# The hi part of each weight block from a rounding DMA in place of a ScalarE copy

## The chip, the cores and the metric

One Trainium2 chip, one of its cores. The metric is the device time of one execution in microseconds (us), as the median of several runs.

## The reference, cut to what matters

Two transformer-like blocks over 1024 tokens of width 1024, in float32. The first puts 16 meta tokens ahead, projects them all, runs three sequence mixers (HGRN2, Mamba2, S5), projects back, and ends in an MLP with a squared ReLU; the second has a gated delta rule, a spatial gating branch and a gated, convolved feed-forward. Around each stand layer norms. The dense products are what fills the time:

```python
proj = h @ w_in[l]                                        # 1040 x 1024 by 1024 x 3078
h = layer_norm(ALPHA * h + mixed @ w_out[l], ...)         # by 1024 x 1024
ff = jnp.square(jax.nn.relu(h @ w_mlp_in[l])) @ w_mlp_out[l]     # by 1024 x 4096 x 1024
proj = x @ w_in_2[l]                                      # by 1024 x 5128
h = gate_a * (o_a @ w_branch_a[l]) + gate_b * (o_b @ w_branch_b[l])
up = causal_depthwise_conv_2(x @ w_up[l], conv_ffn[l])    # by 1024 x 5632
x = ... (jax.nn.silu(a_ff) * b_ff) @ w_down[l]            # by 2816 x 1024
```

(The matrix sizes behind the comment signs are added here; in the kernel the tokens are taken in two halves.)

## The kernel before, in words

**Split operands.** A dense product in float32 is made of three products in float32r, the rounded form that TensorE takes in one pass: each operand is split into a hi part (the rounded value) and a lo part (what the rounding left), and `mm3` adds hi by hi, hi by lo and lo by hi in PSUM. Weights come from DRAM in blocks of 128 partitions by 1024 columns (512 KB; some are 780, 688 or 1032 columns wide). `weights` (line 223 on) does for each block: a DMA on SP's queue into a raw tile `wr` (2 buffers), a ScalarE copy into the float32r tile `wh` (3 buffers), and a VectorE subtraction raw - hi into `wl` (3 buffers):

```python
self.nc.sync.dma_start(raw[:, :w], src)
...
self.act(hi[:, :w], raw[:, :w])
self.tt(lo[:, :w], raw[:, :w], hi[:, :w].bitcast(F32), ALU.subtract)
```

There are 431 such blocks. A block feeds 24 products of 512 columns on TensorE, or about as much work; in the first projection, where some serve both halves, up to 72 shorter ones.

**How blocks are used.** In `fm` (first and second projection, the MLP's and feed-forward's up products, `merge`) a block is one unit: all its products, then the next block. In `down` (the MLP's and the feed-forward's products back to 1024 columns) blocks come in twos: for a group of four hidden tiles and each half `ch` of the output, two blocks A and B (then C and D) are both read in each of the four token tiles t = 0 to 3. With three buffers, C takes a buffer that was free before, while D takes A's, which is not read for the last time before the fourth token tile. There are 26 groups with four hidden tiles: 16 in the two halves of the MLP (`in_wmo`) and 10 in the feed-forward (`in_wdn`); two more have two.

**Stages.** `run` (line 1474 on) interleaves a dense part with the mixers' steps of another half by hand-written rates (`steps`). Roughly: up to 490 us the first projection, the mixers of the first half, its out-projection and the norm; from there to 2800 us the dense parts follow each other, with mixers beside them.

**Queues.** A scheduler orders the instructions of each engine by its own model of times; an engine then runs its list in order, and an instruction that waits holds up all behind it. In the kernel before, loads go on SP's queue, most stores of intermediates to DRAM (`S1`, `vdt`, `Y1`, `Y2`, `gt`, `qkv`, `sg` and the like) on GpSimd's (POOL), where there are also fills and the small power operation of the norms (line 1151). A few small loads are on ScalarE's queue.

Of the kernel before, what the change touches and what calls it, by code (L numbers as in the profile page):

```python
# [17 lines left out]
DRAM = bass.MemoryType.DRAM  # L18
# [6 lines left out]
ALPHA = 2.0 ** 0.25  # L25
# [4 lines left out]
# columns of the constant array  # L30
C_ID = 0
C_I10 = 128                   # 1024 times the identity
C_SGN = C_I10 + 128
C_TRI = C_SGN + 1
C_BLK = C_TRI + 128           # ones in the two diagonal 64-blocks
C_BAND = C_BLK + 128          # 64 zeros, 128 ones, 64 zeros
C_N = C_BAND + 256

# columns of the array of byte masks: the levels (only the columns in the second halves of their blocks),
# the same transposed (only the first halves), the diagonal, what is below it  # L40
# [6 lines left out]
# columns of the per-feature parameter array  # L47
P_HNW = 0
P_LB = 1
P_CW1 = P_LB + 3              # 7 x 4  # L50
# [4 lines left out]
P_CWQ = P_GB + 2              # 12 x 4  # L55
P_DNW = P_CWQ + 48
P_CWF = P_DNW + 1             # 44 x 3
# [4 lines left out]
# columns of the row array (the same on all partitions)  # L62
# [7 lines left out]
# order of the feature-major tiles of the first projection  # L70
U1 = dict(u=0, f=2, q=5, g=8, xbc=11, z=18)
NU1 = 21
# ... and of the second
# [4 lines left out]
class Op:  # L78
    """The hi and lo parts of an operand."""
# [8 lines left out]
class Kb:  # L88
# [54 lines left out]
    def mask(self, o, b=None):  # L143
        """A byte mask for four blocks of 128 columns, or for the halves of a level's blocks in them."""
        n = 128
        if b is not None:
            o += 64 * LEVELS.index(b)
            n = 64
        m = self.bm[:, o:o + n].rearrange("p (o t) -> p o t", o=1).to_broadcast([128, 4, n])
        return m if b is None else m.rearrange("p c (n b) -> p c n b", b=b)  # L150

    def halves(self, x, i, b):
        """The first or second halves of the blocks of 2 b columns."""
# [11 lines left out]
    def t(self, w, dt=F32):  # L165
        """A working tile of the mixers."""
        return self.mx.tile([128, 528], dt, tag="f", bufs=self.NF, name=self.nm("f"))[:, :w]

    def ta(self):
        """Two working tiles of 528 columns, out of the accumulators' tiles."""  # L170
# [16 lines left out]
    # ---------------------------------------------------------------- operands  # L187
# [18 lines left out]
    def xt(self, f=False):  # L206
        """A tile for the hi and lo parts of an operand; f: out of the mixers' tiles."""
# [8 lines left out]
    def split(self, src, w, f=False):  # L216
        """hi and lo parts of src [128, w]."""
# [5 lines left out]
    def weights(self, src, w):  # L223
        """hi and lo parts of a block of weights [128, w] in DRAM."""
# [4 lines left out]
        self.act(hi[:, :w], raw[:, :w])  # L229
# [3 lines left out]
    def mm3(self, out, a, b, start, stop):  # L233
        """out += a^T b with hi and lo parts."""
# [4 lines left out]
    def fm(self, out, w, xs, o, n, k0=0):  # L239
        """out [128 features, n tokens] from a unit of weights and the tiles xs."""  # L240
# [5 lines left out]
    # ---------------------------------------------------------------- first projection  # L246
    def p1(self):
# [21 lines left out]
        def unit(i, hs):  # L269
# [4 lines left out]
            for h in hs:  # L274
                if nme != "u":
                    self.S1[nme, j, h] = self.dram([128, HW[h] + 3], f"s{nme}{j}{h}")
                for o, n in pieces[h] if nme in ("u", "f", "xbc") or h == 1 else ((16, 512),):
# [3 lines left out]
                    if nme == "u":  # L281
# [3 lines left out]
                        nc.gpsimd.dma_start(self.uT[j][:, :, j0:j0 + n // 8],  # L285
# [3 lines left out]
                    nc.gpsimd.dma_start(self.S1[nme, j, h][:, 3 + o:3 + o + n], st[:, :n])  # L289
                    if nme == "xbc" and h == 0:  # L290
                        if o == 0:
                            nc.gpsimd.dma_start(self.S1[nme, j, 0][:, 0:3], self.zeros[:, 0:3])
                        else:
                            self.hx[j] = self.dram([128, 3], f"hx{j}")
                            nc.gpsimd.dma_start(self.hx[j], st[:, n - 3:n])
                    if nme == "xbc" and h == 1:
                        nc.gpsimd.dma_start(self.S1[nme, j, 1][:, 0:3], self.hx[j])
# [3 lines left out]
        def vd(h):  # L301
            tt = [(128 * c + T0[h], 128) for c in range(4)]
            for g in ([(0, 16)] + tt[:2], tt[2:]) if h == 0 else (tt,):
# [9 lines left out]
                for b, (o, n) in zip(bs, g):  # L313
                    st = self.ev()
                    self.act(st[:n, :390], b[:n, :390])
                    nc.gpsimd.dma_start(self.vdt[h][o:o + n, :], st[:n, :390])
# [21 lines left out]
    # ---------------------------------------------------------------- HGRN2  # L338
    def hgrn_pre(self):
        """ln(1 - lb) and lb, a column for each pair of heads."""  # L340
# [13 lines left out]
    def hgrn(self, p, h):  # L354
# [13 lines left out]
        # log f and k  # L368
# [19 lines left out]
        # scores  # L388
# [17 lines left out]
        # the queries of a level for both heads at once, each among zeros for the other's features  # L406
# [40 lines left out]
        # decays  # L447
# [12 lines left out]
        # kd with tokens on the partitions, and what each chunk adds to the state  # L460
# [16 lines left out]
        # the states before the chunks, both heads' on the diagonal  # L477
# [20 lines left out]
        # norm and gate  # L498
# [10 lines left out]
        nc.gpsimd.dma_start(self.Y1[h][p], r)  # L509

    # ---------------------------------------------------------------- Mamba2
    def softplus(self, x, tag, w):
        """max(x, 0) + ln(1 + exp(-|x|)) in place; x is narrow."""
# [6 lines left out]
    def rows(self, x, n):  # L520
        """The sums over tokens up to each, a row in DRAM for each of the n columns of x."""
# [15 lines left out]
    def square(self, x):  # L537
        """The hi and lo parts of the square of x [128, 512]."""
# [7 lines left out]
    def sums(self, out, parts):  # L546
        """The sum of the products of ones (lhsT) and operands (p: their partitions)."""
# [4 lines left out]
    def conv4(self, src, NT, cw, cb, out):  # L552
        """Causal convolution of four taps, then silu."""
# [10 lines left out]
    def mamba(self, h):  # L564
# [8 lines left out]
        # dt and dA, with tokens on the partitions; the first six columns are the short chunk  # L573
# [19 lines left out]
        for c in range(c0, 5):  # L593
            L = 16 if c == 0 else 128
            t0 = 0 if c == 0 else R0 + 128 * (c - 1)
            # acum_t and exp(acum_t) on all partitions
# [24 lines left out]
            # x dt and B with tokens on the partitions  # L621
# [39 lines left out]
        # gate, norm  # L661
# [9 lines left out]
        for j in range(3):  # L671
# [11 lines left out]
            nc.gpsimd.dma_start(self.Y1[h][3 + j], Y[j])  # L683
            yield

    # ---------------------------------------------------------------- S5
    def cmul(self, o, a, b, t):
        """o = a b for pairs (re, im) of access patterns; t: two temporaries of the shape."""
# [7 lines left out]
    def exp(self, out, x, w):  # L696
        """exp(x) to the last bits, for small tiles (w: four times the width of x)."""
# [1016 lines left out]
```

## Time and profile before

| | |
|---|---|
| median of 3 runs | 2840.28 us |
| lowest, highest | 2838.09, 2843.76 us |
| span of the profiled execution | 2831.3 us |
| median less that span | 9.0 us |
| PE (TensorE matmul) busy | 2768.6 us, 98% |
| DVE (VectorE) busy | 1793.7 us, 63% |
| ACT (ScalarE) busy | 1163.4 us, 41% |
| POOL (GpSimd) busy | 220.4 us, 8% |
| the 16 DMA engines, mean | 124 GB/s |

The profiled execution's own device time is not recorded apart from the three runs; its span, from the first to the last instruction, is what the rows below are read from, and 9.0 us is taken as what lies around it. A matmul's duration in a row is from its start to its modelled end, and matmuls overlap: what one costs in a full stretch is the stretch divided by their number.

### The profile page before, as it was taken

The page shows a single profiled execution, that of the slowest core. Times are in us where ns is not written, and L with a number is a line of the kernel's source. Part 1 is how long each engine was busy: PE and PEld are TensorE (multiplying, and loading weights), DVE is VectorE, ACT ScalarE, POOL GpSimd, SP SyncE. Part 2 cuts the span into 40 slices and gives each one's busy share as a digit, 9 for nine tenths or more (in the row PEclk, how much of TensorE's full clock was granted, in tenths as well). Part 3 has the DMA queues.
Part 4 walks back from the last instruction along what each step waited for, and adds up shares of the span by engine and source line. Part 5 has one row for each costly group of instructions (what it writes and reads, how often), then busy time and mean ns, then how long its engine had stood idle before and what let it go on. Part 6 is the DMA issues. An engine that isn't in the chain of part 4 may idle for free.

```text
span 2831.3 us, 37337 instructions
## 1 busy us (share of the span) xinstructions
PE 2768.6 (98%) x14176; PEld 2262.4 (80%) x14176; DVE 1793.7 (63%) x3321; ACT 1163.4 (41%) x1810; POOL 220.4 (8%) x365
## 2 busy tenths in 40 slices
PE   8999999999999999999999999999999999999997
PEld 7788777777878878877788888888788888888886
DVE  7678768777756554386545675535867557675556
ACT  4334344444442353364323334435545334344432
POOL 3121000000001121010000001110100000000000
PEclk9999999999999999999999999999999999999999
DMA  7333462323344444333333455433244433342232
GB/s 220 122 94 93 139 202 81 113 89 113 106 147 149 157 144 133 123 101 123 105 104 119 142 184 166 126 126 130 79 136 140 149 104 101 107 139 92 97 96 75
DMA packets 138036, 351.55 MB, mean 124 GB/s; under 512 B 26779, under 2 KB 40641, under 8 KB 137857
## 3 DMA queue, kind: packets, MB, share of 16 engines
q1 hardware_dynamic: 113712, 295.34, 32.9%
q0 software_dynamic: 16672, 48.50, 5.0%
q10 hardware_dynamic: 7473, 5.34, 0.7%
q8 instruction: 111, 1.82, 0.3%
q14 instruction: 68, 0.56, 0.1%
HBM read 296.84 MB, written 51.69 MB: 123 GB/s over the span
## 4 chain that ended last, share of the span: by engine, by line
PE 81%; issue 7%; DVE 6%; DMA 2%; ACT 2%; POOL 1%; SPq 0%; DVEq 0%; POOLq 0%; ACTq 0%
PE ps L204 73%; PE px L204 7%; DVE f L192 2%; ACT f L189 1%; DVE wl L192 1%; PE px L1265 1%; DVE f L195 1%; DMA hx<-ev 1%; DMA wr<-in_w 0%; DVE acc L195 0%; DMA f<-rows 0%; DVE f L433 0%; ACT wh L189 0%; DVE ta L192 0%; ACT ev L189 0%
## 5 line engine op out<-in xcount | busy, mean ns | idle before, releaser
L204 PE MATMUL ps<-xt,wh 128*128 128x512 f32 (+1 forms) x3616 | 1117.0, 388 | 8.7 <-ACT wh L189 8.5
L192 DVE TENSOR_TENSOR wl<-wr,wh 128x1024 fp32r<-128x1024 f32 (+3 forms) x431 | 521.5, 1210 | 606.7 <-ACT wh L189 590.2
L189 ACT ACTIVATE wh<-wr 128x1024 fp32r<-128x1024 f32 (+3 forms) x431 | 452.3, 1050 | 898.4 <-PE ps L204 826.1
L204 PE MATMUL ps<-wh,xt 128*128 128x512 f32 (+3 forms) x2624 | 813.1, 384 | 4.7 <-ACT xt L189 4.4
L204 PEld LDWEIGHTS ps<-xt,wh 128*128 128x128 f32 x3616 | 665.9, 189 | 141.7 <-ACT wh L189 8.5
L204 PE MATMUL ps<-xt,wl 128*128 128x512 f32 (+1 forms) x1808 | 698.6, 387 | 3.9 <-DVE wl L192 3.9
L204 PEld LDWEIGHTS ps<-wh,xt 128*128 128x128 f32 (+1 forms) x2624 | 485.8, 188 | 99.9 <-ACT xt L189 6.9
L204 PE MATMUL ps<-wl,xt 128*128 128x512 f32 (+3 forms) x1312 | 502.2, 383 | 0.8 <-DVE wl L192 0.7
L204 PEld LDWEIGHTS ps<-xt,wl 128*128 128x128 f32 x1808 | 341.5, 189 | 72.8 <-DVE wl L192 5.5
L204 PE MATMUL ps<-f,wh 128*128 128x512 f32 x960 | 300.5, 394 | 0.0
L204 PEld LDWEIGHTS ps<-wl,xt 128*128 128x128 f32 (+1 forms) x1312 | 246.7, 188 | 46.5 <-DVE wl L192 2.0
L189 ACT ACTIVATE f<-f 128x512 f32<-128x512 f32 (+6 forms) x300 | 178.5, 613 | 200.6 <-DVE f L192 62.3
L204 PE MATMUL px<-f,f 128*128 128x128 f32 (+8 forms) x1832 | 201.4, 258 | 16.8 <-DVE f L192 10.2
L204 PEld LDWEIGHTS ps<-f,wh 128*128 128x128 f32 x960 | 180.3, 188 | 42.3
L189 ACT ACTIVATE ev<-ps 128x512 f32<-128x512 f32 (+4 forms) x303 | 169.6, 561 | 72.9 <-PE ps L204 67.1
L192 DVE TENSOR_TENSOR acc<-acc,ps 128x512 f32<-128x512 f32 x192 | 130.8, 683 | 95.8 <-PE ps L204 93.9
L204 PE MATMUL ps<-f,wl 128*128 128x512 f32 x480 | 189.4, 394 | 0.0
L204 PEld LDWEIGHTS px<-f,f 128*128 128x128 f32 (+2 forms) x1192 | 133.3, 180 | 52.9 <-issue 22.8
L192 DVE TENSOR_TENSOR f<-f,f 128x256 f32<-128x256 f32 (+5 forms) x244 | 128.6, 547 | 39.0 <-ACT f L189 37.0
L189 ACT ACTIVATE xt<-ev 128x512 fp32r<-128x512 f32 x131 | 82.3, 629 | 149.2 <-DVE ev L192 145.9
L195 DVE SCALAR_TENSOR_TENSOR ev<-ev,p,ev 128x512 f32<-128x512 f32 x176 | 132.2, 751 | 2.7 <-ACT ev L189 0.6
L192 DVE TENSOR_TENSOR xt<-ev,xt 128x512 fp32r<-128x512 f32 x124 | 85.9, 696 | 49.6 <-ACT xt L189 49.1
(223 smaller groups left out, 2046.9 us busy)
## 6 DMA issues: line engine op xcount, KB each, us to landing
wr<-in_w SPq DMA_DIRECT2D x93, 512.0 KB, 3.8
wr<-in_wup SPq DMA_DIRECT2D x88, 512.0 KB, 3.5
wr<-in_wmi SPq DMA_DIRECT2D x64, 512.0 KB, 3.6
wr<-in_wmo SPq DMA_DIRECT2D x64, 512.0 KB, 3.6
wr<-in_wdn SPq DMA_DIRECT2D x44, 512.0 KB, 3.5
wr<-in_wo SPq DMA_DIRECT2D x32, 512.0 KB, 3.7
Y<-f POOLq DMA_DIRECT2D x32, 256.0 KB, 2.6
ev<-Y SPq DMA_DIRECT2D x32, 256.0 KB, 3.6
```

Source lines behind the costliest of these rows:

```text
L189: self.nc.scalar.activation(out=out, in_=in_, func=func, **kw)
L192: self.nc.vector.tensor_tensor(out=out, in0=a, in1=b, op=op)
L195: self.nc.vector.scalar_tensor_tensor(out=out, in0=a, scalar=s, in1=b, op0=op0, op1=op1)
L204: self.nc.tensor.matmul(out, lhsT, rhs, start=start, stop=stop)
L1265: nc.tensor.transpose(b[:, 128 * t:128 * t + 128], acc[t][:, 128 * k:128 * k + 128], self.ident)
```

## The change

`weights` fetches the block twice. The raw copy still comes on SP's queue. The hi part is no longer made by ScalarE: a second DMA, on POOL's queue, reads the same block from DRAM and writes it as float32r into `wh`, so that the transfer rounds. VectorE still subtracts. All stores that were on POOL's queue go to SP's. Buffers, loops and rates are as they were; comments and docstrings are taken out.

```diff
         raw = self.wp.tile([128, 1032], F32, tag="wr", bufs=2, name=self.nm("wr"))
         self.nc.sync.dma_start(raw[:, :w], src)
         hi = self.wp.tile([128, 1032], F32R, tag="wh", bufs=3, name=self.nm("wh"))
         lo = self.wp.tile([128, 1032], F32R, tag="wl", bufs=3, name=self.nm("wl"))
-        self.act(hi[:, :w], raw[:, :w])
+        self.nc.gpsimd.dma_start(hi[:, :w], src)
         self.tt(lo[:, :w], raw[:, :w], hi[:, :w].bitcast(F32), ALU.subtract)
...
-                    nc.gpsimd.dma_start(self.S1[nme, j, h][:, 3 + o:3 + o + n], st[:, :n])
+                    nc.sync.dma_start(self.S1[nme, j, h][:, 3 + o:3 + o + n], st[:, :n])
...
-            nc.gpsimd.dma_start(dst[:, o:o + 512], st[:, :512])
+            nc.sync.dma_start(dst[:, o:o + 512], st[:, :512])
```

The other stores (`uT`, `hx`, `vdt`, `Y1`, `Y2`, `X2`, `out`, `sg`, `qkv`) change in the same way.

The scheduler then places things anew. Three places:

**TensorE, `down` of a feed-forward group late in the program.** In the names, `wh_22358`/`wl_22359` are block A, `wh_22426` is C, and `wh_22432`/`wl_22433` are D, which takes A's buffer; `ps_22436`, `ps_22450` and `ps_22464` are the first three token tiles of the second half. In both kernels the last read of A stands 6 products ahead of the first read of C (six reads of B lie between). Before, D's first read follows after six products of C:

```order
L204 MATMUL ps_22436<-wh_22426,xt_21893 128x512
L204 MATMUL ps_22436<-wl_22427,xt_21893 128x512
L204 MATMUL ps_22436<-wh_22426,xt_21893 128x512
L204 MATMUL ps_22436<-wh_22426,xt_22110 128x512
L204 MATMUL ps_22436<-wl_22427,xt_22110 128x512
L204 MATMUL ps_22436<-wh_22426,xt_22110 128x512
L204 MATMUL ps_22436<-wh_22432,xt_22191 128x512
L204 MATMUL ps_22436<-wl_22433,xt_22191 128x512
```

Now there are ten of C ahead of it (the first six are the same as before, and the rows begin with the last of these):

```order
L204 MATMUL ps_22436<-wh_22426,xt_22110 128x512
L204 MATMUL ps_22450<-wh_22426,xt_21893 128x512
L204 MATMUL ps_22450<-wl_22427,xt_21893 128x512
L204 MATMUL ps_22450<-wh_22426,xt_21893 128x512
L204 MATMUL ps_22450<-wh_22426,xt_22110 128x512
L204 MATMUL ps_22436<-wh_22432,xt_22191 128x512
L204 MATMUL ps_22450<-wl_22427,xt_22110 128x512
L204 MATMUL ps_22450<-wh_22426,xt_22110 128x512
L204 MATMUL ps_22450<-wh_22432,xt_22191 128x512
L204 MATMUL ps_22464<-wh_22426,xt_21893 128x512
L204 MATMUL ps_22464<-wl_22427,xt_21893 128x512
L204 MATMUL ps_22436<-wl_22433,xt_22191 128x512
```

So between A's last read and D's first there are now 16 products instead of 12, and between A's last read and the first of D's lo part 22 instead of 13.

**SP's queue, the second projection (`p2`), its gate units.** `wr_...` are raw blocks of `in_w2`, `gt_...` the gates' rows in DRAM. Before, raw loads alone:

```order
L226 DMA wr_10353<-in_w 128x1024
L226 DMA wr_10388<-in_w 128x1024
L226 DMA wr_10443<-in_w 128x1024
L226 DMA wr_10478<-in_w 128x1024
L226 DMA wr_10537<-in_w 128x1024
L226 DMA wr_10596<-in_w 128x1024
```

Now a store stands between each two of them:

```order
L226 DMA wr_10478<-in_w 128x1024
L1344 DMA gt_1724_10293<-ev_10325 128x512
L226 DMA wr_10537<-in_w 128x1024
L1344 DMA gt_1734_10352<-ev_10384 128x512
L226 DMA wr_10596<-in_w 128x1024
L1344 DMA gt_1740_10387<-ev_10419 128x512
L226 DMA wr_10631<-in_w 128x1024
```

The store of the unit whose block is `wr_10388` stands behind the raw load of the fourth block after it.

**POOL's queue, in the feed-forward of the second half, beside a norm.** `lnm_...` are the norm's columns. Before, the power operations stand among each other and the stores of the output:

```order
L1151 TENSOR_TENSOR lnm_21136<-lnm_21136,k 128x1
L1151 TENSOR_TENSOR lnm_21224<-lnm_21224,k 128x1
L1151 TENSOR_TENSOR lnm_21312<-lnm_21312,k 128x1
L1151 TENSOR_TENSOR lnm_21400<-lnm_21400,k 128x1
L1260 DMA out<-acc_14275 128x512
```

Now hi loads stand between them:

```order
L229 DMA wh_21142<-in_wup 128x1024
L1151 TENSOR_TENSOR lnm_21136<-lnm_21136,k 128x1
L229 DMA wh_21180<-in_wup 128x1024
L1151 TENSOR_TENSOR lnm_21224<-lnm_21224,k 128x1
L1151 TENSOR_TENSOR lnm_21312<-lnm_21312,k 128x1
L1151 TENSOR_TENSOR lnm_21400<-lnm_21400,k 128x1
L229 DMA wh_21230<-in_wup 128x1024
```

Each hi load waits for the last product that reads its buffer, and each power operation for VectorE's statistics.

## Rows read from the trace of the kernel before

**Rows 1.** The page, part 1: busy time, share of the span, instructions.
```profile
PE 2768.6 (98%) x14176; PEld 2262.4 (80%) x14176; DVE 1793.7 (63%) x3321; ACT 1163.4 (41%) x1810; POOL 220.4 (8%) x365
```

**Rows 2.** Waits of PE, whole span: total us, times, longest.
```profile
PE px L204 <- DVE f L192: 11.4, 12, 2.8
PE ps L204 <- ACT wh L189: 8.5, 1, 8.5
PE px L204 <- ACT f L189: 6.6, 10, 1.2
PE px L1280 <- ACT acc L189: 5.1, 4, 2.7
PE ps L204 <- DVE wl L192: 4.6, 6, 1.9
PE ps L204 <- ACT xt L189: 4.6, 4, 3.1
...
PE px L204 <- ACT ev L189: 1.4, 1, 1.4
```

**Rows 3.** Windows: length, each engine's busy us (instructions), clock, DMA share, GB/s.
```profile
0.00:70.00 70.00, 58.24 (x348) 52.14 (x349) 54.18 (x228) 30.91 (x50) 22.08 (x41) 0.98 0.74 220
...
420.00:490.00 70.00, 63.03 (x298) 48.66 (x299) 58.70 (x116) 32.69 (x45) 6.99 (x11) 0.93 0.31 98
...
2170.00:2240.00 70.00, 70.00 (x303) 56.63 (x302) 47.57 (x68) 34.87 (x50) 0.00 (x0) 1.00 0.58 188
...
2590.00:2660.00 70.00, 70.00 (x303) 56.60 (x302) 37.97 (x53) 28.15 (x37) 0.00 (x0) 1.00 0.28 91
...
2800.00:2870.00 70.00, 17.00 (x74) 13.45 (x72) 23.23 (x42) 1.06 (x1) 3.70 (x4) 0.92 0.08 30
```

**Rows 4.** Groups by form: busy us, mean ns | idle before, releasers.
```profile
L192 DVE TENSOR_TENSOR wl<-wr,wh 128x1024 fp32r<-128x1024 f32 x401 | 489.9, 1222 | 558.3 <-ACT wh L189 541.7 <-PE px L1265 8.1 <-PE ps L204 3.3
...
L189 ACT ACTIVATE wh<-wr 128x1024 fp32r<-128x1024 f32 x401 | 424.6, 1059 | 829.0 <-PE ps L204 767.0 <-issue 27.5 <-DMA wr<-in_w 9.2
...
L1344 POOL DMA_DIRECT2D gt<-ev x32 | 17.3, 540 | 187.2 <-ACT ev L189 118.4 <-ACT f L189 68.7
```

**Rows 5.** DMA issues: queue, count, KB each, median us from issue to landing.
```profile
wr<-in_wmo SPq DMA_DIRECT2D x64, 512.0 KB, 3.6
wr<-in_wdn SPq DMA_DIRECT2D x44, 512.0 KB, 3.5
...
Y<-f POOLq DMA_DIRECT2D x32, 256.0 KB, 2.6
...
out<-acc POOLq DMA_DIRECT2D x8, 256.0 KB, 2.6
out<-acc SPq DMA_DIRECT2D x8, 256.0 KB, 2.0
...
uT<-ev POOLq DMA_DIRECT2D x4, 132.0 KB, 7.7
```

**Rows 6.** DMA queues: packets, MB, share of 16 engines' span (q0 is POOL's).
```profile
q1 hardware_dynamic: 113712, 295.34, 32.9%
q0 software_dynamic: 16672, 48.50, 5.0%
```

**Rows 7.** Timeline of the start: start us, length us, engine, operation.
```profile
1.63 0.43 SPq L226 DMA_DIRECT2D wr<-in_w  x1
...
7.40 1.06 ACT L189 ACTIVATE wh<-wr 128x1024 fp32r<-128x1024 f32 x1 [2.65 <-DMA wr<-in_w]
...
8.51 1.25 PE L204 MATMUL ps<-xt,wh 128*128 128x264 f32 x4 [8.51 <-ACT wh L189]
...
14.62 0.68 ACT L189 ACTIVATE ev<-ps 128x264 f32<-128x264 f32 x1 [0.90 <-PE ps L204]
...
15.59 0.86 POOL L285 DMA_DIRECT2D uT<-ev  x1 [1.25 <-ACT ev L189]
```

**Rows 8.** Windows of 10 us at the start, columns as in rows 3.
```profile
10.00:20.00 10.00, 9.68 (x68) 9.47 (x69) 7.55 (x25) 6.57 (x15) 5.08 (x9) 1.00 1.06 367
```

More of the change, by code (lines that the diff above doesn't have):

```diff
@@ L284, in unit @@
                         j0 = (HOFF[h] + o) // 8
-                        nc.gpsimd.dma_start(self.uT[j][:, :, j0:j0 + n // 8],
+                        nc.sync.dma_start(self.uT[j][:, :, j0:j0 + n // 8],
                                             st[:, :n].rearrange("p (t j) -> p t j", t=8))
@@ L288, in unit @@
                     self.act(st[:, :n], b[:, :n])
-                    nc.gpsimd.dma_start(self.S1[nme, j, h][:, 3 + o:3 + o + n], st[:, :n])
+                    nc.sync.dma_start(self.S1[nme, j, h][:, 3 + o:3 + o + n], st[:, :n])
                     if nme == "xbc" and h == 0:
                         if o == 0:
-                            nc.gpsimd.dma_start(self.S1[nme, j, 0][:, 0:3], self.zeros[:, 0:3])
+                            nc.sync.dma_start(self.S1[nme, j, 0][:, 0:3], self.zeros[:, 0:3])
                         else:
                             self.hx[j] = self.dram([128, 3], f"hx{j}")
-                            nc.gpsimd.dma_start(self.hx[j], st[:, n - 3:n])
+                            nc.sync.dma_start(self.hx[j], st[:, n - 3:n])
                     if nme == "xbc" and h == 1:
-                        nc.gpsimd.dma_start(self.S1[nme, j, 1][:, 0:3], self.hx[j])
+                        nc.sync.dma_start(self.S1[nme, j, 1][:, 0:3], self.hx[j])
         self.hx = {}
@@ L315, in vd @@
                     self.act(st[:n, :390], b[:n, :390])
-                    nc.gpsimd.dma_start(self.vdt[h][o:o + n, :], st[:n, :390])
+                    nc.sync.dma_start(self.vdt[h][o:o + n, :], st[:n, :390])
                 yield
@@ L508, in hgrn @@
         self.stt(r, r, self.col(P_HNW), g, ALU.mult, ALU.mult)
-        nc.gpsimd.dma_start(self.Y1[h][p], r)
+        nc.sync.dma_start(self.Y1[h][p], r)
     def softplus(self, x, tag, w):
@@ L682, in mamba @@
             self.stt(Y[j], Y[j], self.col(P_NW1 + j), r, ALU.mult, ALU.mult)
-            nc.gpsimd.dma_start(self.Y1[h][3 + j], Y[j])
+            nc.sync.dma_start(self.Y1[h][3 + j], Y[j])
             yield
@@ L946, in glu @@
             self.ts(o, o, 0.5, ALU.mult)
-            nc.gpsimd.dma_start(self.Y1[h][6 + m], o)
+            nc.sync.dma_start(self.Y1[h][6 + m], o)
             yield
@@ L1125, in delta @@
         self.stt(r, r, self.col(P_DNW), z, mult, mult)
-        nc.gpsimd.dma_start(self.Y2[h][hd], r)
+        nc.sync.dma_start(self.Y2[h][hd], r)
         yield
@@ L1176, in spatial @@
             self.act(v, b)
-            nc.gpsimd.dma_start(self.Y2[h][4:8, :, 128 * t:128 * t + 128].rearrange("g p t -> p g t"),
+            nc.sync.dma_start(self.Y2[h][4:8, :, 128 * t:128 * t + 128].rearrange("g p t -> p g t"),
                                 v.rearrange("p (g t) -> p g t", g=4))
@@ L1259, in ln @@
                 if out is not None:
-                    nc.gpsimd.dma_start(out[128 * t:128 * t + 128, c], a)
+                    nc.sync.dma_start(out[128 * t:128 * t + 128, c], a)
                 yield
@@ L1362, in sgu @@
                 self.act(st[:, :344], bs[t][:, :344])
-                nc.gpsimd.dma_start(self.sg[h][128 * t:128 * t + 128, 344 * cg:344 * cg + 344], st[:, :344])
+                nc.sync.dma_start(self.sg[h][128 * t:128 * t + 128, 344 * cg:344 * cg + 344], st[:, :344])
         yield from sgu(2)
@@ L1369, in p2 @@
                     self.S2["qkv", j, hh] = self.dram([128, 515], f"qkv{j}{hh}")
-                nc.gpsimd.dma_start(self.S2["qkv", j, 0][:, 0:3], self.zeros[:, 0:3])
+                nc.sync.dma_start(self.S2["qkv", j, 0][:, 0:3], self.zeros[:, 0:3])
             st = unit(U2["qkv"] + j, self.S2["qkv", j, h], 3)
             if h == 0:
-                nc.gpsimd.dma_start(self.S2["qkv", j, 1][:, 0:3], st[:, 509:512])
+                nc.sync.dma_start(self.S2["qkv", j, 1][:, 0:3], st[:, 509:512])
             yield
```

## The prediction

> **What bounds the kernel now.** I read the busy times first, then the waits of PE, then windows, and last the rows on what the new transfer resembles. PE is busy 2768.6 of 2831.3 us [rows 1], so all that any change can give back is 62.7 us of PE's idle time. PE's waits name a few us each [rows 2]: VectorE's results for the mixers (11.4), ScalarE's (6.6, 5.1, 4.6 and 1.4), and 8.5 for the first hi block. The windows say where: 11.8 us are idle in the first 70 us, 7.0 from 420 to 490, and in the dense stretches from there to 2800 PE runs 303 products in each 70 us without a gap [rows 3]. That gives the unit of this working: 70 / 303 = 0.231 us for a product of 512 columns, 5.55 us for the 24 of a block. It is the same at a DMA share of 0.28 and of 0.58 [rows 3], so more traffic alone does not slow PE. The last 14 us are the final norm.
>
> So the time after is the time before, less idle time that goes, plus new holes in PE's row. A hole comes where a block's hi part is late. The one question is how long it takes from the moment that TensorE lets go of a `wh` buffer to the moment that the next block's hi part is in it (call it L), and how much work PE has in between.
>
> **What is removed.** 431 ScalarE copies, 401 of them at 1.06 us [rows 4], some 452 us of ScalarE's 1163 [rows 1]. Nothing of it is on PE's path but the first one, since PE waits for a `wh` copy once [rows 2]. ScalarE stood blocked ahead of these copies for 829 us, mostly for PE to free a buffer [rows 4]; that goes, and the mixers' ScalarE work behind it comes sooner. PE's waits that name other ScalarE work sum to 6.6 + 5.1 + 4.6 + 1.4 = 17.7 us [rows 2]. ScalarE loses 39% of its work, which would be 7 of them if waits shrank in proportion; most of them are for something ScalarE had itself just been handed, so I take 4. **-4 us**, between 0 and -17.7.
>
> **What is added, beside other work.** 431 transfers, about 223 MB. At the share that the present queues need for a MB, 32.9% / 295.34 [rows 6], this is 25% more, 39% going to 64% on the mean; in the feed-forward, 0.28 to 0.56. That is below what PE has been seen to run beside, so nothing. On POOL one issue takes 0.54 us [rows 4]; 431 of them and without the stores' own it stays under 20% busy. VectorE's lo subtraction is as before, 1.22 us [rows 4]. It stood waiting 558 us for ScalarE's copies [rows 4] and now waits for transfers; what is queued behind it there are the sums into `acc` and the hidden tiles' products, and who waits for those is PE, through four PSUM buffers and, for the hidden tiles, across the first tile of the next group, 11 us. I price this at nothing while L is below some 8 us.
>
> **What is added on the path: the refill of a `wh` buffer.** Before, L was a ScalarE copy, 1.06 us. Now it is the wake-up of POOL, the issue and the transfer. The wake-up: the ScalarE instruction that ends at 14.62 + 0.68 releases a POOL issue that starts at 15.59, so 0.29 us [rows 7]. The transfer: no row shows a rounding one, nor a weight block on POOL's queue. From below, POOL's plain 256 KB store lands in 2.6 us [rows 5]; with another 256 KB, at 0.28 x 5.55 / 2 = 0.78 us of all DMA engines [rows 3], 3.4. From above, the slowest transfer on POOL's queue is that of `uT`, 7.7 us, in very short runs and at the busy start [rows 5]. The nearest row is the same block's raw load, 3.5 to 3.6 us on SP's queue; and the same store takes 2.6 on POOL's and 2.0 on SP's, so 0.6 more [rows 5]. I take 3.5 + 0.6 + 0.29 = **4.4 us**, between 3.7 and 8.0.
>
> Then the cover. Where blocks are used one by one, three buffers leave two blocks between, about 11 us; these need L + 1.22 for the lo part, 5.6, and it is there. The tight place is D in `down`, whose buffer is A's. By the order shown with the change, 16 products lie between A's last read and D's first, 3.70 us, and 22, 5.08 us, ahead of D's lo part. The hi part is late by 4.4 - 3.70 = 0.70 us; the lo part, at 4.4 + 1.22 = 5.6, is then in time, since the hole moves its own turn to 5.8. There are 25 such places among the 26 groups: 18 with 16 products, one with 15 (0.93), four with 17 (0.47), one with 18 (0.24), one with 21. The sum is 12.6 + 0.9 + 1.9 + 0.2 = **+16 us**. At L = 3.7 it is nothing; at 8.0 it is 25 x 4.3 = 107, and then 39 more blocks with about 7.4 us ahead of their lo part are late as well, by 8.0 + 1.2 - 7.4 = 1.8 each, 70 more, and some 10 early. In the first projection four blocks of `wv` and the one behind have about 4.6 us for L + 1.22; they follow each other, so that a hole at one is cover for the next: **+2 us**.
>
> A rule of the Trainium skill speaks against the queue that was chosen: by "SBUF — State Buffer", section "Who interferes with whom", descriptors of a transfer issued from GpSimd can't be written while VectorE holds the port pair that the two share, in certain of its modes. The 32 issues of the row took 540 ns on the mean beside a VectorE that is busy 63% of the span [rows 1, 4], which shows no such hold. If one instruction as long as the lo subtraction (1.22 us) held each of the 25, the sum would be 31 us more, 2888 instead of 2857.
>
> **The start.** POOL has three free `wh` buffers and sends for three blocks at once, ahead of most of the tokens that the first products need. The DMA engines are full there, 367 GB/s [rows 8]; 1.57 MB more is 4.3 us. The first ScalarE copy (1.06 us, from 7.40, with PE's first product at 8.51 [rows 7]) is no longer in the chain. **+3 us**, between -1 and +4.3.
>
> **The stores on SP's queue.** A store waits for ScalarE's result of its unit, and behind it stands a raw load. By the order shown with the change that load is for the fifth block on, more than 20 us ahead, against 3.6 us of landing and 1.22 of subtraction. Nothing; without that lead it would cost up to 5 us a unit in the two projections. POOL's power operations now stand among hi loads; a load behind three of them can be late by their wait, beside norms only, and I count it to the spread.
>
> **The sum.** -4 + 16 + 2 + 3 = +17 us on the span, 2848; with the 9 us by which the median stands above the span, **2857 us**, 0.6% slower.
>
> **Rivals.**
> 1. *Hidden anyway (2841 us).* If the rounding transfer lands in the 3.4 us worked out above from the half-sized store, L is 3.7 and D is just in time; what is left is 2 + 3 - 4. For it: the order leaves 16 products where there were 12, as if made for such an L. Against: loads of this size land later than that even on SP's queue. The Trainium skill gives the same outcome: "DMA: Bandwidth & Descriptors", section "Anatomy of one DMA — SWDGE (gpsimd) path", has 2.0 us + bytes / 436 GB/s, an estimate of 3.2 us for a block and no hole; its 2.6 for 256 KB agrees with the store's row.
> 2. *Faster (2828 us).* The transfer is hidden and ScalarE, no longer blocked ahead of its copies, lets the mixers run ahead: all 17.7 us of its waits go, against 5 of start and first projection, 2840 - 13. It decides if the mixers of the first 490 us wait for ScalarE rather than VectorE. Against it: VectorE is busy 58.7 of 70 us there, ScalarE 32.7 [rows 3].
> 3. *The rounding is slow (3000 us).* No row excludes that a rounding transfer moves at half the rate of a plain one or less. At half, a block takes 1.55 us more, L is 6, D is late by 2.25: 56 us for 25, near 2900. At a third, the feed-forward needs 0.28 + 0.84 of the DMA engines, over 1, and PE follows them, 12% on that stretch and its like. At L = 8.0 it is 2840 + 187 + 3, about 3030.
>
> **How the numbers follow.** Within 0.2% (5.7 us) a measurement of this kernel can't tell a difference from none: 2834.6 to 2846. The forecast has 0.52, with a range of its own of 2846 (L = 4) to 2910 (L = 6); hidden 0.17; faster 0.11; slow 0.20. So faster 0.11, same 0.17, slower 0.72. The range from 2834 leaves out the 0.11 below; 2960 leaves out about half of the slow case above.
>
> **What would show it.** Rounding transfers landing in about 4 us from issue. PE waiting for `wh` transfers some 25 times, 0.7 us each, all in `down`, and next to nothing elsewhere after 490 us. ScalarE near 700 us, VectorE's wait at the lo subtraction naming a DMA. If `wh` lands in 3.4 and PE does not wait, rival 1; if it takes 6 or more and PE waits in `fm` too, rival 3. If raw loads land late behind stores and PE waits for `wl` in the projections, the cover of the stores was wrong.

## The result: 143 us slower

The changed kernel takes 2982.91 us (median of 4 runs, 2981.02 to 2993.99) against 2840.34 for the kernel before (4 runs, 2838.09 to 2843.76): a ratio of 1.0514, 95% interval 1.0493 to 1.0534. The forecast was 2857, its range 2834 to 2960. The sign was right, the size was not; the term that gave the sign, PE's waits for late hi parts in `down`, comes to some 21 of the 143 us (below), so most of the loss has another cause.

The page of the changed kernel: busy times as in [rows 1], queues as in [rows 6].

```profile
span 2981.8 us, 37424 instructions
...
PE 2808.9 (94%) x14176; PEld 2277.9 (76%) x14176; DVE 1801.4 (60%) x3321; ACT 753.4 (25%) x1379; POOL 306.6 (10%) x544
...
q1 hardware_dynamic: 158336, 343.84, 36.0%
q0 software_dynamic: 62064, 223.51, 25.9%
```

The span grew by 150.5 us. PE's idle time went from 62.7 to 172.9 us, +110. PE's busy time for the same products went from 2768.6 to 2808.9, +40; its mean granted clock over the whole span is 0.980, where it was 0.992, and 1.2% of 2800 us, an estimate, is 34 of the 40. Where the holes are, the clock is lower: from 420 to 490 us, columns as in [rows 3], it is 0.85 with PE busy 53.8 us of 70, where it was 0.93 with 63.0. A mean of 0.85 is, by estimate, 21 of the 70 us at the lower of its two levels (1.2 GHz) and the rest at the upper (2.4 GHz). The changed kernel is by then some 27 us behind, so the stretch holds other work; over the same work, in the windows further down, the clock is 0.97, 0.98 and 0.99 where it was 0.98, 0.99 and 0.99.

```profile
420.00:490.00 70.00, 53.75 (x207) 40.38 (x207) 36.91 (x67) 23.53 (x42) 5.62 (x11) 0.85 0.62 188
```

Where it went is read from windows whose edges are the same pieces of PE's work in both kernels (the start of the first product and of two later ones, found by their count). Columns as in [rows 3]. Before:

```profile
0.00:403.00 403.00, 375.75 (x2402) 322.08 (x2402) 297.41 (x897) 164.05 (x301) 66.04 (x124) 0.98 0.46 138
403.00:2316.00 1913.00, 1891.91 (x9603) 1535.23 (x9603) 1168.98 (x1931) 795.97 (x1240) 143.75 (x226) 0.99 0.40 127
2316.00:2831.00 515.00, 500.95 (x2176) 405.06 (x2174) 327.32 (x494) 203.37 (x270) 10.65 (x16) 0.99 0.31 102
```

After:

```profile
0.00:430.50 430.50, 379.73 (x2402) 324.62 (x2402) 298.39 (x897) 125.01 (x257) 34.95 (x70) 0.97 0.64 179
430.50:2453.50 2023.00, 1925.46 (x9600) 1548.35 (x9599) 1173.30 (x1930) 510.94 (x939) 218.69 (x379) 0.98 0.64 197
2453.50:2981.00 527.50, 503.71 (x2178) 404.92 (x2176) 329.72 (x495) 117.44 (x183) 52.98 (x95) 0.99 0.59 187
```

The last stretch, dense products with few mixers beside them, loses 12.5 us. The middle, where mixers run beside the dense parts, loses 110, and the first 430 us lose 27.5. PE's waits, columns as in [rows 2], say the same:

```profile
PE px L204 <- ACT f L189: 38.6, 21, 7.5
PE px L204 <- DVE f L192: 35.1, 23, 5.1
PE ps L204 <- DVE wl L192: 14.7, 13, 2.2
PE ps L204 <- DMA wh<-in_wmo: 11.4, 14, 2.5
PE ps L204 <- DMA wh<-in_w: 9.8, 2, 8.7
PE ps L204 <- DMA wh<-in_wdn: 9.6, 7, 3.9
```

The waits for `wh` of `in_wmo` and `in_wdn` are the holes that the prediction counted, 21.0 us; of the 9.8 for `in_w`, 8.7 are the first block, which cost 8.5 before as well [rows 2]. The two largest, 73.7 us where they were 18.0, are not: they are products into `px`, the mixers' PSUM banks. PE runs its list in order, the mixers' products stand in it among the dense ones, and when a mixer's operand is late the dense product behind it is late as well.

One such hole, the timeline of the changed kernel from 428 to 440 us (start, length, engine, operation, idle time before):

```profile
429.19 0.53 POOL L229 DMA_DIRECT2D wh<-in_wo  x1 [8.56 <-PE ps L204]
429.27 0.40 SPq L665 DMA_DIRECT2D f<-sz  x1
...
429.44 2.20 PE L204 MATMUL px<-f,o 64*128 64x512 f32 x6 [0.55 <-ACT f L189]
...
434.54 0.63 ACT L189 ACTIVATE f<-f 128x512 f32<-128x512 f32 x1 [4.76 <-DMA f<-sz]
436.05 1.22 DVE L192 TENSOR_TENSOR wl<-wr,wh 128x1024 fp32r<-128x1024 f32 x1 [5.94 <-DMA wh<-in_wo]
437.20 0.68 DVE L192 TENSOR_TENSOR f<-f,f 128x512 f32<-128x512 f32 x1
...
437.91 1.15 ACT L189 ACTIVATE f<-f 128x512 f32<-128x512 f32 x2 [2.75 <-DVE f L192]
...
439.09 0.69 DVE L192 TENSOR_TENSOR f<-f,f 128x512 fp32r<-128x512 f32 x1 [1.22 <-ACT f L189]
...
439.11 2.38 PE L204 MATMUL px<-f,o 128*128 128x512 f32 x4 [7.47 <-ACT f L189]
```

PE stands from 431.64 to 439.11. Mamba2 loads its gate (`f<-sz`, sent at 429.27); it is there at 434.5, ScalarE takes 0.63 us, and the multiplication on VectorE could begin at 435.17. But in VectorE's list the lo subtraction of an out-projection block stands before it, and that waits until 436.05 for a hi transfer sent at 429.19. So the multiplication begins at 437.20, 2.0 us late, and everything behind it too. The other 5.4 us are the load, 5.3 us from its issue until ScalarE goes on, and the steps behind it; the load was sent 0.08 us after a hi block of 512 KB.

The kernel before has a hole at the same place, of 3.06 us, from 404.29 to 407.35:

```profile
400.64 0.38 SPq L665 DMA_DIRECT2D f<-sz  x1
...
405.51 0.63 ACT L189 ACTIVATE f<-f 128x512 f32<-128x512 f32 x1 [1.82 <-DMA f<-sz]
...
407.21 1.13 ACT L189 ACTIVATE f<-f 128x512 f32<-128x512 f32 x2
407.35 0.80 PE L204 MATMUL ps<-wh,xt 128*128 128x512 f32 x1 [3.06 <-ACT xt L189]
```

There the load took 4.9 us until ScalarE went on, hardly less, and ScalarE's last step ended 7.7 us after the load's issue, where it is 9.8 now. That is 2.1 of the 4.4 us by which the hole grew. The other 2.3 go with the order: the next product in PE's list was then a dense one, which didn't need this chain, and is now the mixer's.

The transfers themselves, columns as in [rows 5]:

```profile
wh<-in_w POOLq DMA_DIRECT2D x93, 512.0 KB, 5.0
...
wh<-in_wmo POOLq DMA_DIRECT2D x64, 512.0 KB, 4.4
wr<-in_wmo SPq DMA_DIRECT2D x64, 512.0 KB, 4.4
...
wh<-in_wdn POOLq DMA_DIRECT2D x44, 512.0 KB, 4.4
...
gt<-ev SPq DMA_DIRECT2D x32, 256.0 KB, 5.3
```

### The profile page after: what moved, and what is told of

Same layout as the page of the kernel before. It is cut to its first block, busy times and chain, and to the rows that moved or that the text cites. A ratio compares the mean times of both kernels' runs of the same rounds, so it can differ in the third digit from the quotient of the medians.

```text
span 2981.8 us, 37424 instructions
## 1 busy us (share of the span) xinstructions
PE 2808.9 (94%) x14176; PEld 2277.9 (76%) x14176; DVE 1801.4 (60%) x3321; ACT 753.4 (25%) x1379; POOL 306.6 (10%) x544
## 3 DMA queue, kind: packets, MB, share of 16 engines
q0 software_dynamic: 62064, 223.51, 25.9%
## 4 chain that ended last, share of the span: by engine, by line
issue 50%; PE 24%; DMA 11%; DVE 9%; POOL 5%; ACT 1%; SPq 0%; POOLq 0%; DVEq 0%; ACTq 0%
PE ps L204 21%; POOL wh L229 4%; PE px L204 2%; DVE f L192 2%; DVE wl L192 2%; DMA wh<-in_w 1%; DMA wh<-in_wmo 1%; DMA wh<-in_wdn 1%; DVE acc L195 1%; DVE f L195 1%; DMA ev<-in_ln 1%; DMA wh<-in_wsg 1%; DVE ta L192 1%; DMA f<-in_xT 1%; DVE acc L192 1%
## 5 line engine op out<-in xcount | busy, mean ns | idle before, releaser
L204 PE MATMUL ps<-wh,xt 128*128 128x512 f32 (+3 forms) x2624 | 826.9, 389 | 30.8 <-DMA wh<-in_wmo 11.4
L204 PEld LDWEIGHTS ps<-wh,xt 128*128 128x128 f32 (+1 forms) x2624 | 491.8, 190 | 137.0 <-DMA wh<-in_wmo 17.6
L229 POOL DMA_DIRECT2D wh<-in_w x93 | 49.6, 534 | 611.2 <-PE ps L204 545.5
L189 ACT ACTIVATE f<-px 128x256 f16<-128x256 f32 (+8 forms) x164 | 68.9, 428 | 166.3 <-PE px L204 114.7
```

Source lines behind the costliest of these rows:

```text
L189: self.nc.scalar.activation(out=out, in_=in_, func=func, **kw)
L204: self.nc.tensor.matmul(out, lhsT, rhs, start=start, stop=stop)
L229: self.nc.gpsimd.dma_start(hi[:, :w], src)
```

## The experiments

Three theories were on record before the first runs: A, the hi part is late and VectorE, in order, stands at the lo subtraction for it; B, the stores on SP's queue hold up the loads behind them; C, the extra bytes make every transfer land later. A fourth, D, came later: the order that the scheduler gave TensorE and VectorE is a cost by itself. Ratios are against runs of the kernel before on the same chip (2836 to 2838 us; 2840 in the runs of the result, so a difference in us between runs on different chips is sure only to some 4 us).

### The two halves of the change, each alone

From the kernel before, e1 (this store and all others):

```diff
-        nc.gpsimd.dma_start(self.Y1[h][p], r)
+        nc.sync.dma_start(self.Y1[h][p], r)
```

From the kernel before, e2:

```diff
-        self.act(hi[:, :w], raw[:, :w])
+        self.nc.gpsimd.dma_start(hi[:, :w], src)
```

> The kernel before with one part of the change alone: all stores on SP's queue, the hi part still a ScalarE copy. Theory A (the hi part is late: VectorE, in order, stands at the lo subtraction until the transfer has landed, and the raw loads and mixer loads on SP's queue stand behind that): this part costs little, 2835 to 2870 us. Theory B (the stores, each waiting for a unit's result, hold up the raw loads and the mixers' loads behind them on SP's queue): most of the 143 us are here, 2920 to 2980. Theory C (the extra 223 MB of traffic makes every transfer land later): nothing here, 2835 to 2850.

> The kernel before with the other part alone: the hi part by the rounding transfer on POOL's queue, stores left on POOL's queue. Theory A (hi late): 2940 to 3000 us, or more, since the hi loads now also stand behind stores. Theory B (stores on SP): 2845 to 2890, since SP's queue is as before. Theory C (traffic): 2940 to 2990.

Stores on SP alone: 2835.12 us, 0.9988 (0.9979 to 0.9998). The hi transfer alone: 2996.00 us, 1.0556 (1.0527 to 1.0585). Theory B falls: over the whole run the stores cost nothing, and all of the loss, 13 us more than all of it, is the hi transfer. A and C both allowed about this much, so the run doesn't choose between them.

### Is rounding slow?

From the changed kernel, e4:

```diff
-        self.nc.gpsimd.dma_start(hi[:, :w], src)
+        self.nc.gpsimd.dma_start(hi[:, :w], src.bitcast(F32R))
```

> The changed kernel with the hi transfer as a plain copy of the same bytes on the same queue (no rounding, so hi is the whole value and lo is zero); the order of all engines is the same row for row. If the rounding itself costs transfer time: hi lands earlier than 4.4 to 5.0 us and the time falls by 20 us or more. If not (all of A, B, C): 2975 to 2995 us and the same landing times within 0.2 us.

2979.98 us, 1.0501 (1.0486 to 1.0517), as the changed kernel. A plain transfer lands as late as a rounding one (4.1 to 5.4 us against 4.4 to 5.1). No cost of rounding is seen here.

### VectorE does not wait for the hi transfer

From the changed kernel, e3:

```diff
-        self.tt(lo[:, :w], raw[:, :w], hi[:, :w].bitcast(F32), ALU.subtract)
+        self.tt(lo[:, :w], raw[:, :w], raw[:, :w], ALU.subtract)
```

> The changed kernel, but the lo subtraction reads the raw block twice (raw - raw, so the lo part is zero and is left out of the result in effect): VectorE does the same instruction of the same size and no longer waits for the hi transfer; TensorE still does. Theory A: most of the loss goes, 2850 to 2900 us, and raw loads on SP's queue are early again. Theory B and theory C: nothing changes, 2965 to 2990.

2900.61 us, 1.0216 (1.0201 to 1.0231): 82 us are gone with one operand. That is theory A, at the upper end of what it gave, but 64 us over the kernel before stay, and the scheduler had ordered the engines anew, so part of the gain could be the order's.

### A hi buffer more, and a buffer of each kind more

From the changed kernel, e6 (`NF` is the number of the mixers' working tiles, which give the room):

```diff
-    NF = 24
+    NF = 22
...
-        hi = self.wp.tile([128, 1032], F32R, tag="wh", bufs=3, name=self.nm("wh"))
+        hi = self.wp.tile([128, 1032], F32R, tag="wh", bufs=4, name=self.nm("wh"))
```

The same edit from the changed kernel (e7) and from the kernel before (e8):

```diff
-    NF = 24
+    NF = 18
...
-        raw = self.wp.tile([128, 1032], F32, tag="wr", bufs=2, name=self.nm("wr"))
+        raw = self.wp.tile([128, 1032], F32, tag="wr", bufs=3, name=self.nm("wr"))
...
-        hi = self.wp.tile([128, 1032], F32R, tag="wh", bufs=3, name=self.nm("wh"))
-        lo = self.wp.tile([128, 1032], F32R, tag="wl", bufs=3, name=self.nm("wl"))
+        hi = self.wp.tile([128, 1032], F32R, tag="wh", bufs=4, name=self.nm("wh"))
+        lo = self.wp.tile([128, 1032], F32R, tag="wl", bufs=4, name=self.nm("wl"))
```

> The changed kernel with a fourth wh buffer (two of the mixers' 24 working tiles give the room; the kernel before with 22 has the same order of instructions on every engine). The hi transfer is then sent for a block earlier, some 5.5 us, more than the 4.4 to 5.0 us it takes, and VectorE and TensorE should find it landed. Theory A: 2850 to 2905 us, VectorE's waits at the lo subtraction naming TensorE and not the hi transfer. Theory C: 2960 to 2990, the traffic being the same.

> The changed kernel with one more buffer of each kind (wr 3, wh 4, wl 4; 18 of the mixers' working tiles). The raw load no longer waits for the subtraction just done, the lo part can be made a block earlier, so VectorE's subtraction need not wait for anything. Theory A: 2835 to 2880 us, below the run with a fourth wh buffer alone. Theory C: 2890 or more, since the bytes are the same.

> The kernel before with the same buffers (wr 3, wh 4, wl 4; 18 working tiles): what the deeper buffers give without the change. 2815 to 2840 us by every theory; against it the run of the changed kernel with these buffers is to be read.

With a fourth hi buffer 2887.66 us, 1.0181 (1.0156 to 1.0206). With one more of each kind 2949.07, 1.0392 (1.0369 to 1.0414): more buffers, and most of the gain gone. The kernel before with these buffers 2832.71, 0.9980 (0.9971 to 0.9989). The expectation for e7 was wrong, and its trace shows what VectorE waits for. VectorE's waits at the lo subtraction (columns as for PE's waits), the largest of the changed kernel:

```profile
DVE wl L192 <- DMA wh<-in_wup: 109.3, 63, 4.9
DVE wl L192 <- DMA wh<-in_w: 100.6, 31, 8.7
```

Of e6:

```profile
DVE wl L192 <- PE ps L204: 433.5, 204, 7.4
...
DVE wl L192 <- DMA wh<-in_wmi: 54.9, 28, 4.8
DVE wl L192 <- DMA wh<-in_wup: 39.9, 16, 4.6
```

Of e7:

```profile
DVE wl L192 <- DMA wh<-in_w: 122.8, 37, 7.6
DVE wl L192 <- DMA wh<-in_wup: 103.6, 57, 5.0
```

In e6 the hi transfer runs a block ahead of the lo buffer, and what VectorE mostly waits for is PE, to let go of that buffer. In e7 there are as many lo buffers as hi buffers again, both come free with the same block, and VectorE waits for a transfer that has just been sent. So these rows speak for the lead of the transfer over the instruction that reads it, and not for the number of buffers. The two runs differ in the order of TensorE and VectorE and in the working tiles as well (18 of them cost the kernel before nothing, by e8), so how much of the 61 us between them is the lead alone wasn't shown.

### The bytes alone

The hi part by ScalarE and stores on SP, as in e1; each finished hi block is also sent to a scratch array that nobody reads (e5), or its first 8 columns are (e12).

```diff
         self.tt(lo[:, :w], raw[:, :w], hi[:, :w].bitcast(F32), ALU.subtract)
+        self.nc.gpsimd.dma_start(self.scr[self.nsc % 8][:, :w], hi[:, :w].bitcast(F32))
```

In e12 that line is:

```diff
+        self.nc.gpsimd.dma_start(self.scr[self.nsc % 8][:, :8], hi[:, :8].bitcast(F32))
```

> Traffic alone: the hi part by ScalarE as before and stores on SP's queue as in the run with that part alone (2835 us); added is a transfer of each finished hi block to a scratch array in DRAM on POOL's queue, which nobody reads: 431 transfers, 223 MB, as many bytes as the hi loads of the change. Theory A (the hi part is late and VectorE waits for it): 2835 to 2860 us. Theory C (traffic makes all transfers land later, and that costs the 65 us which were left when VectorE no longer waited): 2880 to 2910, with loads and stores landing 1 us or more later than in the run with stores on SP alone.

> The run with added traffic (2884 us), its 431 added transfers cut from the whole hi block to its first 8 columns (4 KB in place of 512); the order of the engines is nearly the same. Theory C as narrowed (the bytes delay the other transfers): 2833 to 2850 us, loads back at 3.5 to 4.0. If it is the issues on POOL, the waits or the order that cost there: 2870 to 2890.

2884.09 us, 1.0169 (1.0152 to 1.0186), with the bytes; 2844.53, 1.0029 (1.0018 to 1.0041), without. The order of instructions is nearly the same in these two, so 40 us are the 222 MB between them; 9 more over e1 go with the 431 small transfers, TensorE's order being e1's. The bytes act on the other transfers. DMA issues, columns as in [rows 5], of e5:

```profile
scr<-wh POOLq DMA_DIRECT2D x401, 512.0 KB, 3.4
wr<-in_w SPq DMA_DIRECT2D x93, 512.0 KB, 4.9
...
gt<-ev SPq DMA_DIRECT2D x32, 256.0 KB, 3.8
```

Of e12:

```profile
scr<-wh POOLq DMA_DIRECT2D x431, 4.0 KB, 1.8
...
wr<-in_w SPq DMA_DIRECT2D x93, 512.0 KB, 4.0
...
gt<-ev SPq DMA_DIRECT2D x32, 256.0 KB, 2.2
```

A mean share of 0.60 (0.42 in e12) leaves the DMA engines free 40% of the time, and yet a store of 256 KB lands 1.6 us later. Over a few us the share is far from its mean, here in e5 (columns as in [rows 3]):

```profile
1502.00:1505.00 3.00, 3.00 (x15) 2.44 (x14) 1.14 (x2) 1.66 (x2) 0.53 (x1) 1.00 0.00 0
...
1509.00:1511.00 2.00, 2.00 (x10) 1.60 (x10) 0.00 (x0) 0.85 (x1) 0.00 (x0) 1.00 1.01 410
```

Transfers are sent in bunches, and those of a bunch share engines that are full: in the hole of the changed kernel shown above the share is 1.01 from 430 to 436 us.

```profile
430.00:436.00 6.00, 1.64 (x5) 0.61 (x5) 0.11 (x1) 0.63 (x1) 0.00 (x0) 0.79 1.01 297
```

The added bytes of e5 go from SBUF to DRAM and those of the change the other way, so that the same 40 us apply to the change is taken over, not measured.

### The order

The scheduler gives TensorE and VectorE other orders in the changed kernel. On VectorE 290 of the 431 lo subtractions stand later among the others than before, 38 earlier, 2.2 rows later on the mean. To tell an order from what it was made for, the instructions of an engine were chained in the order of another kernel (issue order only, no waits; `own` are an engine's instructions as the program makes them, `x` comes from a table of the other kernel's order):

```diff
         Kb(tc, es, ap).run()
+        pin(tc, tc.nc)
...
+            at += x + 1
+            if prev is not None:
+                tc.add_manual_dep(own[at], prev.name, info, reason="pin")
+            prev = own[at]
```

e9 is e1 (hi by ScalarE, stores on SP) in the order of the changed kernel; e10 is e3 in that order; e11 is the changed kernel in the order of the kernel before; e13 is e6 in the order of the changed kernel; e14 is e1 with VectorE alone chained.

> The kernel with stores on SP's queue and the hi part by ScalarE (2835 us), with TensorE's and VectorE's instructions chained (issue order only, no waits added) in the order that the scheduler gave them in the changed kernel. Theory A (waiting for the hi transfer) and theory C (traffic): neither is here, so 2835 to 2860 us. Theory D (the scheduler's new order of TensorE and VectorE is itself the loss): 2900 or more.

> The run in which the subtraction reads the raw block twice (2901 us), with TensorE and VectorE chained in exactly the order of the changed kernel, so that only the wait for the hi transfer is gone from VectorE. Theory A: about as without the chain, 2885 to 2915 us, some 80 below the changed kernel. Theory D: 2960 to 2990, what was gained there having come from the other order.

> The changed kernel with TensorE and VectorE chained in the order of the kernel before. Theory A: no better than the changed kernel, 2975 us or more, since the transfer takes as long and D in `down` has 12 products of cover in place of 16 (25 places with some 0.9 us more each: 3000). Theory D: 2850 to 2930.

> The changed kernel with a fourth wh buffer (2888 us in its own order), TensorE and VectorE chained in the order of the changed kernel. The hi transfer is early here and no copies stand on ScalarE. If that order itself costs the 69 us seen with ScalarE's copies: 2920 to 2960 us. If those 69 us came from the copies standing on ScalarE in an order made without them: 2880 to 2900.

> The kernel with stores on SP's queue and the hi part by ScalarE (2835 us), VectorE alone chained in the order of the changed kernel, TensorE's left to the scheduler. If the cost of that order (2905 with both chained) is VectorE's place for the lo subtraction and its waits: 2885 to 2915 us. If it is where TensorE's mixer products stand: 2835 to 2855.

| | us | ratio (95%) |
|---|---|---|
| e9, hi by ScalarE, order of the changed kernel | 2905.04 | 1.0242 (1.0227 to 1.0257) |
| e10, VectorE doesn't wait, same order as the changed kernel | 2928.55 | 1.0329 (1.0313 to 1.0344) |
| e11, changed kernel in the order of before | 3256.94 | 1.1470 (1.1436 to 1.1504) |
| e13, fourth hi buffer, same order as the changed kernel | 2921.61 | 1.0291 (1.0276 to 1.0307) |
| e14, hi by ScalarE, VectorE alone in the changed order | 2854.03 | 1.0052 (1.0037 to 1.0068) |

For e9 the number is D's; for e10 neither A's nor D's; for e11 D's is refuted, and A's 3000 is far too small. e13 and e14 came out where an order that costs by itself, and TensorE's part in it, had been put. In an order made for a quick hi part, the transfer costs 420 us (e11 against before), three times what was measured: PE waits there 82.9 us for VectorE's `f` and 47.0 for the lo part.

```profile
PE px L204 <- DVE f L192: 82.9, 34, 7.1
PE ps L204 <- DVE wl L192: 47.0, 31, 8.8
```

The new order takes 274 of these back (e11 to the changed kernel). It is not free either: with the hi part quick again it costs 70 us (e9 against e1), and with the hi transfer a block ahead 34 (e13 against e6). In e9 VectorE stands at steps that wait for ScalarE's `ev`, 2.0 and 8.0 us in the kernel before:

```profile
DVE ev L195 <- ACT ev L189: 128.4, 76, 4.9
DVE ev L192 <- ACT ev L189: 120.3, 48, 7.7
```

VectorE's order alone accounts for 19 of the 70 us (e14), and there these two waits are as long, 128.2 and 106.4 us; so it isn't their sum that costs. The rest needs TensorE's order as well: PE's waits for the mixers' operands, 14.0 us for ScalarE's `f` and 7.5 for VectorE's in e1, are 28.0 and 18.1 in e9.

At one and the same order of these two engines the wait can now be priced: without VectorE's 2928.55 (e10), or with the transfer a block ahead, so that TensorE waits less for it too, 2921.61 (e13), against 2982.91. That is 54 us for VectorE's wait alone and 61 for both, not 82. ScalarE's and SP's lists were left to the scheduler and differ in some 50 rows each from the changed kernel's. No run chains a kernel in its own order, so a cost of the chaining itself is not excluded by a run.

### A version that beats both

The edits of e1 and e8 together, from the kernel before:

```diff
-    NF = 24
+    NF = 18
...
-        nc.gpsimd.dma_start(self.Y1[h][p], r)
+        nc.sync.dma_start(self.Y1[h][p], r)
```

> The kernel before with what did not hurt: stores on SP's queue (ratio 0.9988 alone) and deeper buffers (wr 3, wh 4, wl 4, 18 working tiles; 0.998 alone), the hi part by ScalarE. By every theory 2825 to 2835 us, 0.2 to 0.4% below before, and below the changed kernel by the whole 145.

2826.44 us, 0.9962 (0.9949 to 0.9974), some 11 us below the kernel before: the half of the change that costs nothing, deeper buffers, and the hi part left to ScalarE.

## Why the prediction was wrong, by its own steps

**The account of the loss,** taken off one after the other: 61 us for waiting for the hi part, VectorE's wait and TensorE's (changed kernel to e13, same order), 34 for the order (e13 to e6), and 40 for the bytes, which were measured on another kernel (e5 to e12) and are added on the assumption that they cost the same here. Together 135 of the 148 us between the changed kernel and e1. The 13 that are left weren't told apart; the start is among them. The shares depend on the way taken: by e9 the order comes first with 70 us, then 24 for the bytes and TensorE's own waits, less what it gives that ScalarE's copies are gone (e9 to e10), then 54 for VectorE's wait (e10 to the changed kernel).

**The step that failed** is the first conclusion: "A hole comes where a block's hi part is late." It left out that a hole comes as well where a mixer's operand is late, because PE takes the mixers' products in order. The row for it was there: PE waited longest for VectorE's `f` even before, 11.4 us [rows 2], in a kernel with PE busy 98% of the time. From it three terms were set at nothing.

- *VectorE's wait at the lo subtraction, "at nothing while L is below some 8 us".* L came out at about 5 and the wait costs 54 us, 61 with TensorE's. The cover named there was that of the sums into `acc` and of the hidden tiles; the mixers' steps queued on VectorE were not among them. The sum of the waits would not have shown it: VectorE's idle time ahead of the full-width subtraction is 601 us now and was 558 [rows 4]:

```profile
L192 DVE TENSOR_TENSOR wl<-wr,wh 128x1024 fp32r<-128x1024 f32 x401 | 490.4, 1224 | 601.0 <-DMA wh<-in_wup 109.3 <-DMA wh<-in_w 100.6 <-issue 74.7
```

  Of a wait in an ordered list, its end counts for what is queued behind it, and the sum of waits doesn't tell that.
- *The traffic, "nothing".* Its size was right: the two queues take 25.9 + 36.0 = 61.9% of the DMA engines and all queues 63, forecast 64. The price was read from dense stretches at a share of 0.28 and 0.58 [rows 3], where PE runs 303 products either way; that holds for the dense products, which have a lead, and not for a mixer's store and load, which have none. It is 40 us, as far as e5 shows.
- *The order.* It was read for the cover of D alone, as something the change brings at no price. It hides 274 us and costs 34 to 70.

**Terms that held, or were off in size.** L = 4.4 us, 3.7 to 8.0: the hi loads land 4.4 to 5.1 us after issue, and with the wake-up of 0.29 us [rows 7] ahead of it L is 4.7 to 5.4, somewhat above the forecast. D in `down`: +16 us in 25 places forecast; PE's waits for `wh<-in_wmo` and `wh<-in_wdn` sum to 11.4 + 9.6 = 21.0 in 21, the step that was worked out best. Stores on SP's queue at nothing: right over the whole run, by e1. ScalarE's freed time, -4 us: no gain is seen, since PE's wait for ScalarE's `f` is 38.6 us where it was 6.6; in the hole shown above ScalarE has less to do and is handed it later. What its freed time gives by itself wasn't measured. The start, +3 us and at most 4.3: too small. PE is busy 49.1 us of the first 70, where it was 58.2 [rows 3], and the token loads that the first products need are later:

```profile
0.00:70.00 70.00, 49.12 (x296) 44.33 (x297) 35.73 (x151) 18.84 (x36) 8.02 (x18) 0.93 0.89 252
...
f<-in_xT SPq DMA_DIRECT2D x8, 264.0 KB, 9.9
```

They took 6.5 us before. The bound had taken the DMA engines' time for three more blocks once; these blocks went ahead of the tokens. The stores have a part in it, which the prediction had put at nothing: with them alone on SP's queue (e1) PE is busy 54.0 us there, 4.3 us less than before, and stores of `uT` stand ahead of token loads in SP's list.

```profile
0.00:70.00 70.00, 53.97 (x324) 48.52 (x325) 41.47 (x179) 29.65 (x48) 4.13 (x12) 0.95 0.77 201
```

How much of the 27.5 us of the first stretch is this wasn't measured by itself.

**The rivals.** Rounding slow: false, by e4; that its 3000 us was nearest is luck, since the loss has other causes. Faster: false. Hidden anyway: false, with hi loads that land in 4.4 to 5.1 us. By "DMA: Bandwidth & Descriptors", section "Anatomy of one DMA — SWDGE (gpsimd) path", in the Trainium skill a block was estimated at 3.2 us. The 4 KB transfers of e12 land in 1.8 us, near the fixed 2.0 of that page of the Trainium skill; the 512 KB ones take 4.4 to 5.1; in e5, where they go the other way, from SBUF to DRAM, 3.4. The other page of the Trainium skill weighed there, "SBUF — State Buffer", section "Who interferes with whom", has issues on POOL held up by VectorE in certain of its modes. The issues of the hi loads took 528 to 537 ns on the mean, by group, where the stores took 540 [rows 4]:

```profile
L229 POOL DMA_DIRECT2D wh<-in_w x93 | 49.6, 534 | 611.2 <-PE ps L204 545.5 <-DVE f L192 23.7 <-PE px L204 16.8
```

No hold is seen; whether VectorE was in such a mode beside them, no row tells.

**The range.** Its upper number for L = 6, 2910, isn't what the prediction's own terms give: 25 places with some 2.2 us each are 55, which makes 2897, as its third rival has it ("near 2900").

## What to carry to other kernels

When an operation moves from an engine to a transfer, its result comes some microseconds later after the buffer is free, and the price is set by what stands in order behind the instruction that reads it, up to the bottleneck's own list; ask which chains reach the bottleneck with no lead. Here a lead for the transfer (a buffer more for it than for its reader's output) gave back 95 us, and deeper buffers all round 34. Where a scheduler orders the program, a changed latency is three changes: the wait, the order, and what the order was made for; chaining the old or the new order tells them apart.

## What the runs showed of the hardware that was not expected

- A transfer that rounds float32 to float32r lands as a plain one does, 4.4 to 5.1 against 4.1 to 5.4 us for 512 KB, at the same share of the DMA engines (25.9 and 25.8% for 223.51 MB).
- 222 MB more (e5 against e12), from a mean share of 0.42 to 0.60, cost 40 us, though the mean leaves 40% of the DMA engines' time free; the median store of 256 KB went from 2.2 to 3.8 us, in the changed kernel to 5.3.
- Holes in PE's row cost clock as well. Over the whole span it is 0.992 before with 63 us idle, 0.980 in the changed kernel with 173, and 0.948 in e11 with 352, where PE is busy 2906.1 us for the same products that took 2768.6. The idle sum alone doesn't set it: e13 has 0.980 with 126 us idle, e4 0.985 with 177.
